# A gated conv-MLP's up-projection in a hybrid decoder layer: a seventh pair of weight tiles by half-size products, two granules of the down-projection's left operands parked in DRAM, and the last gate's loads and sums scheduled one by one

## The chip, the cores and the metric

The kernel runs on one core of a Trainium2 chip. The metric is device time in microseconds (us), the median of several runs. One execution was also recorded by the hardware profiler; all durations, idle times and clocks below come from that record. PE is TensorE, DVE is VectorE, ACT is ScalarE, POOL is GpSimd, SP is SyncE, which here only issues DMAs. A weight load of TensorE is listed as an engine of its own, PEld.

## The reference

One decoder layer in float32: 512 time steps, model width 1024, MLP width 2816. The change is in the second half:

```python
x = x + gate1 * mixer(adaln(x, c))           # HGRN2 and NSA heads, output projection
h = adaln(x, c)                              # rmsnorm, scale and shift from c @ w_ada + b_ada
u = causal_dwconv(h @ w_up, conv_w, conv_b)  # 1024 -> 2 x 2816, width-3 convolution in time
g = silu(u[..., :2816]) * u[..., 2816:]
x = x + gate2 * (g @ w_down)                 # 2816 -> 1024; gate2 is the sixth adaLN vector
```

`causal_dwconv` is `y[t] = b + u[t-2] w[0] + u[t-1] w[1] + u[t] w[2]` for each channel. The vector gate2 (1024 numbers) is one sixth of `c @ w_ada + b_ada`.

## The kernel before

**Products.** Each float32 product is made of three products of the short float type fp32r: an operand is split into `hi`, its rounded copy (ACT), and `lo`, the remainder (a subtraction, DVE), and `mm3` adds `hi*hi`, `hi*lo` and `lo*hi` (lines 155 to 157). Thus a float32 product is three matmuls.

**The up-projection.** `w_up` has 44 tiles of 128 output channels over K = 1024, which is 8 blocks of 128. Tiles are numbered so that 2f is a gate tile and 2f+1 the value tile with the same channels. A *plain* tile is 8 blocks x 3 = 24 matmuls with 512 columns (all time steps), into a PSUM bank `u`. A *pair* of tiles can also be made together by seven products of half size: K is cut into two halves, time into two halves of 256, the pair gives two tiles, and so the pair is a product of 2 x 2 blocks, for which seven block products do instead of eight. Each is 4 blocks x 3 = 12 matmuls with 256 columns, 84 for the pair, with sums and differences of the weights (tiles `wq`, `w3`) and of the activations (`hS`) as operands. DVE makes these differences; ACT and DVE split them; and between the products DVE adds what the banks share (tokens V, W, lines 1761 and 1763).

**Units.** `UNIT` is an order of tokens, written by hand, for four tiles: one pair by half products (P1 to P7) and two whole tiles (B0 B1 and C0 C1). The other tokens stand for one step each: `p` the post-processing of a finished tile (`up_post`: ACT scales and shifts at line 1623, two DVE additions of shifted copies at 1624 and 1625, ACT's silu at 1628 or DVE's multiplication at 1631); `n`, `f`, `s` the sums and splits of the next pair's weights; `m` the forms of whole tiles; `x` one step of a work list that prepares the left operands of the down-projection (`step(1)`); `g` one step of the generator `ada_last`, which computes gate2. A token with a prime is done for the next unit. `PRO` is the same kind of list for the first eight tiles. The loop runs `for j in range(NB, NU + 1)`, with `NB` = 2: units 2 to 7, tiles 8 to 31. In the last unit the primed tokens do nothing, but for two that prepare the first plain tiles. Tiles 32 to 43 are plain. `PLAIN` has a word for each of them: an A says that a tile prepared then is made with an accumulating transfer (below), and the last figure is how many steps of `ada_last` follow the tile.

**Loads.** `take` keeps three raw weight buffers filled (tag `raw`, 512 KB or 1 MB each); SP issues the next load when a buffer is freed, in program order, so loads wait behind each other. All SP loads go in one queue.

**The accumulating transfer.** Two of the whole tiles' `lo` parts per unit aren't made by DVE: ACT writes a negated copy (line 1684), POOL issues a DMA that adds the raw weights to it (line 1685), and PE uses the result as `wlo`.

**The last gate.** `ada_last` computes gate2 in two halves of 512. For each, it loads 8 blocks of `w_ada` of 128 x 512 (`ada2r`, 256 KB) with SP and adds each, weighted by a column of `cs`, to an accumulator (DVE, line 1407, the last of a half at 1410), then splits that and sums it over the 128 partitions with two small matmuls. Each `next(ada2)` runs up to the next `yield`: a sum of the previous block together with the load of the next.

**The down-projection** follows at about 565 us, also with products saved by sums of blocks. Its left operands come from `g`, in 11 granules j of two tiles. Each has parts `gP[j]` and `gQ[j]` (512 KB each, `hi` and `lo`), kept in SBUF, and `st34` and `st22`, which are written to DRAM (`pk34`, `pk22`) by ACT's DMA queue in `park` (lines 1835 and 1836) and read back by SP later (`load_s34`, line 1881). The first of its three phases calls `each_a(k)` behind every product k.

Of the kernel before, what the change touches and what calls it, by code (L numbers as in the profile page):

```python
# [10 lines left out]
F32 = mybir.dt.float32  # L11
F32R = mybir.dt.float32r
# [4 lines left out]
ALU = mybir.AluOpType  # L17
# [3 lines left out]
P = 128  # L21
# [3 lines left out]
KT = D // P  # L25
# [13 lines left out]
SCRATCH = 1024  # L39
LAG = 4  # L40
NB = 2
NU = 7
CUT = {"B": 6, "C": 7}
ADD = (1, 1)
PLAIN = "1 A3 A2 0 0 3 A2 2 A2 0 1 1"
PRO = ("t t g x M1 M2 t t t t F3 M3 F4 t A5 q0 M4 q1 q2 F6 q3 M5 M6 A7 x q4 g x q5 x t x n1' ns' f2' nc' n5' q6 na' g s4' m0' x x M7 m1' x f6' f7' x x x x f4'")
UNIT = ("P1 S P5 w n1' ns' x f3 B0 P6 P2 B1 x f2' V nc' n5' h1 x p-1 f4' P7 x m0' P3 h0' W p2 p0 na' C0 P4 x x x C1 s4' p1 x m1' x f6' x x x f7'")
PREP = ('sq2 sq3 rq2 rq3', '', 'nq0', 'fq0', 'nq1', '', 'lq0', 'fq1', 'nq2', '', 'lq1', 'fq2', 'nq3', 'lq2', 'fq3',
        'lq3', 'sk0 rk0 sk1 rk1', 'nk0 fk0 sk2 rk2', 'nk1 fk1 sk3 rk3', 'lk0 nk2 fk2', 'lk1 nk3 fk3 sa0 ra0',
        'sa1 ra1 lk2 na0 fa0', 'sa2 ra2 lk3 na1 fa1', 'sa3 ra3 la0 na2 fa2', '', 'la1 na3 fa3', '', 'la2', '', 'la3',  # L50
# [60 lines left out]
def hybrid_layer_kernel(ctx: ExitStack, tc: tile.TileContext, d: dict, out: bass.AP, dbg=None):  # L111
    nc = tc.nc
    ve, sc, gp, pe, sp = nc.vector, nc.scalar, nc.gpsimd, nc.tensor, nc.sync
# [7 lines left out]
    hbm = ctx.enter_context(tc.tile_pool(name="hbm", bufs=1, space=bass.MemoryType.DRAM))  # L121
# [4 lines left out]
    def nm(s):  # L126
        uid[0] += 1
        return f"{s}_{uid[0]}"

    def G(shape, dt=F32, s="g"):  # L130
        return gran.tile([P] + list(shape), dt, tag="g", name=nm(s))
# [4 lines left out]
    def TMP(shape, dt=F32, tag="tmp"):  # L136
        n = 1
        for a in shape[1:]:
            n *= a
        if n > 256:  # L140
            return tp.tile(shape, dt, tag="t2", name=nm(tag), bufs=9)
        return tp.tile(shape, dt, tag="t1", name=nm(tag), bufs=4)
# [4 lines left out]
    def f32(ap):  # L147
        return ap.bitcast(F32)
# [219 lines left out]
    cs = cst.tile([P, 8], F32, name="cs")  # L368
# [1026 lines left out]

    def ada_last(s, res):
        for q in range(2):
            acc = TMP([P, 512], tag="ada2")
            c0 = s * D + q * 512
            gp.memset(acc, 0.0)  # L1400
            sp.dma_start(acc[0:1], d["b_ada"][:, c0:c0 + 512])
            for k in range(KT):
                raw = TMP([P, 512], tag="ada2r")
                sp.dma_start(raw, ada_view[:, k, c0:c0 + 512])
                if k:
                    yield
                    ve.scalar_tensor_tensor(acc, last, cs[:, k - 1:k], acc, ALU.mult, ALU.add)
                last = raw
            yield
            ve.scalar_tensor_tensor(acc, last, cs[:, k:k + 1], acc, ALU.mult, ALU.add)  # L1410
            hi = TMP([P, 512], F32R, tag="rhi")
            lo = TMP([P, 512], F32R, tag="rlo")
            split(hi, lo, acc)
            yield
            ps = PS()
            pe.matmul(ps, onesr, hi, start=True, stop=False)
            pe.matmul(ps, onesr, lo, start=False, stop=True)
            sc.copy(res[:, q * 512:(q + 1) * 512], ps)
            yield


    x1 = []
# [183 lines left out]
    def up_mm(st, sl, ks=range(KT)):  # L1606
        if st not in us:
            us[st] = PS("u")
            if st not in wts:
                wts[st] = next_parts(st < nst - 2, added=st >= 4 * NU + 4 and PLAIN.split()[st - 4 * NU - 4][0] == "A")  # L1610
        hi, lo = wts[st]
# [4 lines left out]
    def up_post(st, silu=True):  # L1616
        f, s = divmod(st, 2)
        u = us.pop(st)
        if st >= 4 * NU + 3:
            step(3)  # L1620
# [94 lines left out]
    def banks(j):  # L1715
        us[4 * j + 1] = PS("u")
        us["x", j] = PS("ux")
        us[4 * j] = (held.pop if j == NU else held.get)(0)

# [5 lines left out]
    def do(j, tok):  # L1725
        last = j == NU
        if tok.endswith("'"):
# [66 lines left out]
    gQ = {}  # L1794
    evens = {}
    work = []
    h1, h2 = slice(0, 256), slice(256, 512)
    pk34 = hbm.tile([P, NJ, 2, 2, 256], F32, name="pk34")
    pk22 = hbm.tile([P, NJ, 2, 256], F32, name="pk22")

    def step(n):

        for _ in range(min(n, len(work))):
            fn, *a = work.pop(0)
            fn(*a)
# [26 lines left out]
                     (park, j, st22, st34)])  # L1832

    def park(j, st22, st34):
        sc.dma_start(pk22[:, j], f32(st22))
        sc.dma_start(pk34[:, j], f32(st34))

# [40 lines left out]
    def load_s34(j):  # L1878
        if j < NJ:
            S34[j] = G([2, 2, 256], F32R, s="S34")  # L1880
            sp.dma_start(f32(S34[j]), pk34[:, j])

    def load_a22(q):
        n = min(2, NJ - 2 * q)
# [42 lines left out]
    ada2 = ada_last(5, gt2)  # L1927
# [26 lines left out]
    made[0] = 1  # L1954
    for tok in PRO.split():
        if tok[0] == "M":
# [12 lines left out]
    made[0] = 1  # L1969
    for j in range(NB, NU + 1):  # L1970
        for tok in UNIT.split():
            do(j, tok)
    assert not tw
    first = 4 * NU + 4
    for st in range(first, nst):
# [5 lines left out]
        elif st > first + 1:  # L1981
            up_post(st - 2)
        for _ in range(int(PLAIN.split()[st - first][-1])):
            next(ada2, None)
# [29 lines left out]
    def each_a(k):  # L2014
        if k == 0:
            sc.activation(ys[nst - 2], ys[nst - 2], AF.Silu)
        elif k == 1:
            up_post(nst - 1)
        elif k % 2:
            step(3)  # L2020
        else:
            load_s34(k // 2 - 1)

# [27 lines left out]
    for q in range(NQ):  # L2051
        w = ready.pop(0)
# [7 lines left out]
    for a in range(2):  # L2060
        t = TMP([P, T])
        ve.tensor_tensor(t, bR[a], gt2[:, lead], ALU.mult)
        ve.tensor_tensor(rest[2 + a][:, lead], rest[2 + a][:, lead], t, ALU.add)
    for bank, a, cols in ((bS[0], 0, lead), (bS[1], 1, slice(0, 256)), (bV[0], 1, slice(256, 512))):
        for n, (hi, lo, j) in enumerate(ws):
            mm3(bank[:, cols], *stat(4, j, a), hi[:, cols], lo[:, cols], n == 0, n == len(ws) - 1)
        t = rest[2 + a][:, cols]
# [23 lines left out]
```

## Time and profile before

| | |
|---|---|
| median of 3 runs | 675.55 us (675.5 to 675.63) |
| the profiled execution, its own time | 675.78 us |
| its span, first to last instruction | 674.0 us |
| mean granted TensorE clock | 0.999 |
| up-projection's units, first to last matmul | 372.70 to 499.18 us |
| plain tiles | 499.18 to 565.38 us |
| HBM traffic | 103.96 MB read, 12.85 MB written |

A row of a timeline gives the start, the duration, the engine, the line of the code, the operation and its output and input; idle time of that engine just before it and what ended it stand in brackets. Matmuls overlap, so that a matmul's duration is longer than the distance to the next one. A row of windows gives, for each stretch, its length, then the busy time of each engine with the number of instructions, the granted clock, the DMA engines' busy share, and GB/s.

### The profile page before, as it was taken

What the parts mean: (1) busy time and instruction counts of PE and PEld (TensorE: products, weight loads), DVE (VectorE), ACT (ScalarE), POOL (GpSimd) and SP (SyncE); (2) the same over time, 40 slices, a digit from 0 to 9 for tenths busy, and PEclk for the clock granted to TensorE, in tenths of its full rate; (3) what the DMA queues carried; (4) which work ended last, traced back from release to release, by engine and by line L of the source; (5) the groups of instructions that cost most, each with busy time, mean ns of one, the idle gap of its engine ahead of it and who ended that gap; (6) DMA issues with size and microseconds to landing.
All of it is one profiled execution on the core that took longest, in us unless ns stands there. A gap on an engine that the chain in (4) does not pass through costs nothing.

```text
span 674.0 us, 10784 instructions
## 1 busy us (share of the span) xinstructions
PE 667.3 (99%) x3965; PEld 564.6 (84%) x3965; DVE 572.7 (85%) x1143; ACT 391.2 (58%) x751; POOL 60.0 (9%) x80
## 2 busy tenths in 40 slices
PE   8999999999999999999999999999999999999997
PEld 4668798788898889888998888989888888888886
DVE  5588988999998997687878988889888799988787
ACT  5564446666677688335665776667655555453431
POOL 1006144200000000200000011010101000000000
PEclk9999999999999999999999999999999999999999
DMA  9998444388042132435437567786689873959932
GB/s 284 284 323 266 143 157 136 104 287 256 10 148 95 33 107 103 167 103 154 156 94 188 150 172 178 205 231 168 160 222 224 247 248 135 377 205 399 382 111 93
DMA packets 109897, 126.43 MB, mean 188 GB/s; under 512 B 7003, under 2 KB 84627, under 8 KB 109845
## 3 DMA queue, kind: packets, MB, share of 16 engines
q1 hardware_dynamic: 103253, 105.84, 50.6%
q0 software_dynamic: 2448, 8.91, 7.0%
q10 hardware_dynamic: 4144, 10.99, 4.2%
q8 instruction: 31, 0.51, 0.3%
q14 instruction: 21, 0.17, 0.1%
HBM read 103.96 MB, written 12.85 MB: 173 GB/s over the span
## 4 chain that ended last, share of the span: by engine, by line
PE 89%; SPq 4%; DVE 3%; DMA 2%; issue 0%; ACT 0%; POOL 0%; DVEq 0%; POOLq 0%
PE u L156 11%; PE u L157 11%; PE u L155 11%; PE dn L156 5%; PE dn L157 5%; PE dn L155 5%; PE pT L155 3%; PE pT L157 3%; PE pT L156 3%; PE F L1056 3%; PE oT L1084 3%; SPq L316 2%; PE oh L157 2%; PE oh L155 2%; PE oh L156 2%; PE lev L1185 2%
## 5 line engine op out<-in xcount | busy, mean ns | idle before, releaser
L155 PE MATMUL u<-h2h,whi 128*128 128x512 f32 (+1 forms) x216 | 81.1, 375 | 0.0
L156 PE MATMUL u<-h2l,whi 128*128 128x512 f32 (+1 forms) x216 | 80.9, 375 | 0.0
L157 PE MATMUL u<-h2h,wlo 128*128 128x512 f32 (+1 forms) x216 | 80.7, 374 | 0.0
L152 DVE TENSOR_TENSOR wlo<-raw,whi 128x1024 fp32r<-128x1024 f32 (+1 forms) x37 | 43.3, 1170 | 6.9 <-ACT whi L151 6.7
L1624 DVE SCALAR_TENSOR_TENSOR y<-u,cv,y 128x511 f32<-128x511 f32 x44 | 32.8, 745 | 17.8 <-ACT y L1623 17.8
L157 PEld LDWEIGHTS u<-h2h,wlo 128*128 128x128 f32 x216 | 40.7, 188 | 7.7 <-DVE wlo L152 0.4
L155 PEld LDWEIGHTS u<-h2h,whi 128*128 128x128 f32 x216 | 40.8, 189 | 6.4
L156 PEld LDWEIGHTS u<-h2l,whi 128*128 128x128 f32 x216 | 40.8, 189 | 6.2
L151 ACT CAST whi<-raw 128x1024 fp32r<-128x1024 f32 (+1 forms) x37 | 37.2, 1005 | 14.9 <-PE kva L157 5.3
L1024 ACT ACTIVATE pt<-pt,mx 128x128 f32<-128x128 f32 (+3 forms) x64 | 35.9, 562 | 11.8 <-DVE mx L1008 10.8
L155 PE MATMUL pT<-hT,whi 128*128 128x512 f32 x96 | 39.2, 408 | 0.0
L157 PE MATMUL pT<-hT,wlo 128*128 128x512 f32 x96 | 37.7, 393 | 0.0
L156 PE MATMUL pT<-hT,whi 128*128 128x512 f32 x96 | 37.6, 391 | 0.0
L1628 ACT ACTIVATE y<-y 128x512 f32<-128x512 f32 x21 | 13.3, 632 | 39.8 <-DVE y L1625 39.8
L1008 DVE CUSTOM_DVE_ANT_0 pt<-S,cmask 128x128 f32<-128x128 f32 (+3 forms) x64 | 29.6, 484 | 6.4 <-PE S L1003 6.3
L1625 DVE SCALAR_TENSOR_TENSOR y<-u,cv,y 128x510 f32<-128x510 f32 x44 | 32.9, 748 | 1.6
L1063 ACT COPY pT<-F 128x512 f32<-128x512 f32 (+2 forms) x52 | 25.9, 502 | 14.4 <-PE F L1056 11.2
L1623 ACT ACTIVATE y<-u,cv 128x512 f32<-128x512 f32 x44 | 33.9, 772 | 0.2 <-PE u L157 0.2
L392 POOL TENSOR_TENSOR hrs<-hrs,mhalf 128x4 f32<-128x4 f32 (+2 forms) x16 | 20.0, 1258 | 136.4 <-DVE hrs L391 136.3
L156 PE MATMUL u<-h2l,w 128*128 128x512 f32 (+1 forms) x88 | 30.0, 341 | 0.0
L155 PE MATMUL u<-h2h,w 128*128 128x512 f32 (+1 forms) x88 | 30.0, 341 | 0.0
L157 PE MATMUL u<-h2h,w 128*128 128x512 f32 (+1 forms) x88 | 30.0, 341 | 0.0
(453 smaller groups left out, 2043.3 us busy)
## 6 DMA issues: line engine op xcount, KB each, us to landing
raw<-in_w_up SPq DMA_DIRECT2D x44, 512.0 KB, 5.1
aw<-in_w_ada SPq DMA_DIRECT2D x24, 512.0 KB, 3.6
raw<-in_w_down SPq DMA_DIRECT2D x10, 1024.0 KB, 5.5
ada<-in_w_ada SPq DMA_DIRECT2D x32, 256.0 KB, 6.1
wlo<-raw POOLq DMA_DIRECT2D x16, 512.0 KB, 5.1
raw<-in_w_in SPq DMA_DIRECT2D x7, 1024.0 KB, 6.3
rawd<-in_w_down SPq DMA_DIRECT2D x12, 512.0 KB, 10.2
pk<-st ACTq DMA_DIRECT2D x11, 512.0 KB, 3.1
```

Source lines behind the costliest of these rows:

```text
L151: sc.copy(hi, src)
L152: (eng or ve).tensor_tensor(lo, src, f32(hi), ALU.subtract)
L155: pe.matmul(o, ah, bh, start=start, stop=False, skip_group_check=True)
L156: pe.matmul(o, ah, bl, start=False, stop=False, skip_group_check=True)
L157: pe.matmul(o, al, bh, start=False, stop=stop, skip_group_check=True)
L1008: ve.tensor_tensor_reduce(pt[:, sl], ps[:, sl], cmask[:, 512 - W:512], -1.0, 1e30, ALU.add, ALU.min, mx[:, e:e + 1])
L1024: sc.activation(pt[:, sl], pt[:, sl], AF.Exp, bias=mx[:, e:e + 1], scale=-1.0, accum_out=su[:, h % 2, e:e + 1])
L1056: pe.transpose(ps[:, j * P:(j + 1) * P], src[:, j * P:(j + 1) * P], ident)
L1063: sc.copy(pT, ps[:, 0:n * P])
L1623: sc.activation(y, u, AF.Identity, bias=cv[:, 132 + c:133 + c], scale=cv[:, 88 + c:89 + c])
L1624: ve.scalar_tensor_tensor(y[:, 1:], u[:, :T - 1], cv[:, 44 + c:45 + c], y[:, 1:], ALU.mult, ALU.add)
L1625: ve.scalar_tensor_tensor(y[:, 2:], u[:, :T - 2], cv[:, c:c + 1], y[:, 2:], ALU.mult, ALU.add)
```

## The change

`NU` goes from 7 to 8: seven units, with tiles 8 to 35, and eight plain tiles, 36 to 43.

`AWAY = (0, 1)`: in `park`, the granules `gQ[0]` and `gQ[1]`, too, are written to DRAM (`pk26`) by ACT's queue and let go. They are read back by SP in the first phase of the down-projection, behind the products k = 3 and k = 5 (`load_away`).

`ada_last` adds directly into the result `gt2`, and a `g` is now either a load or a sum, not both. `PRO` has three more `g`, `UNIT` two (one that loads, behind P7, and one that sums, between p2 and p0), `PLAIN` four words less.

```diff
-NU = 7
+NU = 8
+AWAY = (0, 1)
...
-PLAIN = "1 A3 A2 0 0 3 A2 2 A2 0 1 1"
+PLAIN = "1 A2 A2 2 A2 2 1 1"
...
-UNIT = ("P1 S P5 w n1' ns' x f3 B0 P6 P2 B1 x f2' V nc' n5' h1 x p-1 f4' P7 x m0' P3 h0' W p2 p0 na' C0 P4 x x x C1 s4' p1 x m1' x f6' x x x f7'")
+UNIT = ("P1 S P5 w n1' ns' x f3 B0 P6 P2 B1 x f2' V nc' n5' h1 x p-1 f4' P7 x g m0' P3 h0' W p2 g p0 na' C0 P4 x x x C1 s4' p1 x m1' x f6' x x x f7'")
...
     def ada_last(s, res):
         for q in range(2):
-            acc = TMP([P, 512], tag="ada2")
+            acc = res[:, q * 512:(q + 1) * 512]
...
                 sp.dma_start(raw, ada_view[:, k, c0:c0 + 512])
-                if k:
+                yield
+                ve.scalar_tensor_tensor(acc, raw, cs[:, k:k + 1], acc, ALU.mult, ALU.add)
+                if k < KT - 1:
                     yield
-                    ve.scalar_tensor_tensor(acc, last, cs[:, k - 1:k], acc, ALU.mult, ALU.add)
-                last = raw
-            yield
-            ve.scalar_tensor_tensor(acc, last, cs[:, k:k + 1], acc, ALU.mult, ALU.add)
...
-            sc.copy(res[:, q * 512:(q + 1) * 512], ps)
-            yield
+            sc.copy(acc, ps)
...
     def park(j, st22, st34):
+        if j in AWAY:
+            sc.dma_start(pk26[:, AWAY.index(j)], f32(gQ.pop(j)))
         sc.dma_start(pk22[:, j], f32(st22))
...
+    def load_away(n):
+        if n < len(AWAY):
+            gQ[AWAY[n]] = G([2, 2, 256], F32R, s="gQ")
+            sp.dma_start(f32(gQ[AWAY[n]]), pk26[:, n])
...
         elif k % 2:
             step(3)
+            load_away(k // 2 - 1)
```

**Ahead of the first unit.** On DVE, the operands of the first unit's pair are split and summed: `wq` and `w` are weight forms, `e` is a sum of weights, `gP` a granule, `u` the bank sum of token V. Before:

```order
L152 TENSOR_TENSOR st_800_4165<-s_793_4146,st_800_4165 128x512
L152 TENSOR_TENSOR wq_4322<-raw_4094,wq_4322 128x512
L152 TENSOR_TENSOR w_831_4357<-raw_4245,w_831_4357 128x512
L1670 TENSOR_TENSOR e_4360<-raw_4245 128x512
L152 TENSOR_TENSOR wq_4364<-raw_4094,wq_4364 128x512
```

Now, on DVE at the same place (`gt` is the accumulator of gate2):

```order
L153 TENSOR_TENSOR st_798_4163<-s_791_4144,st_798_4163 128x512
L1407 SCALAR_TENSOR_TENSOR gt_3613<-ada2r_4264,cs,gt_3613 128x512
L153 TENSOR_TENSOR wq_4321<-raw_4092,wq_4321 128x512
L153 TENSOR_TENSOR w_829_4356<-raw_4243,w_829_4356 128x512
L1668 TENSOR_TENSOR e_4359<-raw_4243 128x512
L153 TENSOR_TENSOR wq_4364<-raw_4092,wq_4364 128x512
```

A sum of gate2 stands ahead of four operands that the first unit needs.

**In the units.** On DVE, the second unit, tokens W, p2 and p0 (`u` are banks, `y` the post-processed tiles). Before:

```order
L1763 TENSOR_TENSOR u_4550<-u_4550,w5u_4577 128x256
L1624 SCALAR_TENSOR_TENSOR y_4697<-u_4592,cv,y_4697 128x511
L1625 SCALAR_TENSOR_TENSOR y_4697<-u_4592,cv,y_4697 128x510
L1624 SCALAR_TENSOR_TENSOR y_4702<-u_3874,cv,y_4702 128x511
L1625 SCALAR_TENSOR_TENSOR y_4702<-u_3874,cv,y_4702 128x510
```

Now, on DVE:

```order
L1761 TENSOR_TENSOR u_4553<-u_4553,w5u_4580 128x256
L1622 SCALAR_TENSOR_TENSOR y_4703<-u_4596,cv,y_4703 128x511
L1623 SCALAR_TENSOR_TENSOR y_4703<-u_4596,cv,y_4703 128x510
L1407 SCALAR_TENSOR_TENSOR gt_3613<-ada2r_4680,cs,gt_3613 128x512
L1622 SCALAR_TENSOR_TENSOR y_4709<-u_3875,cv,y_4709 128x511
L1623 SCALAR_TENSOR_TENSOR y_4709<-u_3875,cv,y_4709 128x510
```

One sum stands between the two post-processings. SP's queue in the first units read `raw` loads alone before; now it is, on SP:

```order
L223 DMA raw_4267<-in_w_up 128x8x128 x2
L223 DMA raw_4353<-in_w_up 128x8x128 x2
L1405 DMA ada2r_4451<-in_w_ada 128x512
L223 DMA raw_4453<-in_w_up 128x8x128 x2
L223 DMA raw_4582<-in_w_up 128x8x128 x2
L1405 DMA ada2r_4680<-in_w_ada 128x512
L223 DMA raw_4682<-in_w_up 128x8x128 x2
```

One load of gate2's weights has come in for each unit, behind its two loads of 1 MB.

**In the down-projection's first phase.** On SP (`S` are the read-back sums `st34`, `rawd` and `raw` the weights). Before:

```order
L1881 DMA S_1089_6279<-pk_3610 128x1024
L222 DMA rawd_6293<-in_w_down 128x1024
L1881 DMA S_1095_6319<-pk_3610 128x1024
L222 DMA raw_6333<-in_w_down 128x2x1024
L222 DMA raw_6337<-in_w_down 128x2x1024
L1881 DMA S_1103_6366<-pk_3610 128x1024
```

Now, on SP:

```order
L1882 DMA S_1092_6340<-pk_3610 128x1024
L223 DMA rawd_6354<-in_w_down 128x1024
L1887 DMA gQ_6365<-pk_3612 128x1024
L1882 DMA S_1099_6382<-pk_3610 128x1024
L223 DMA raw_6396<-in_w_down 128x2x1024
L223 DMA raw_6400<-in_w_down 128x2x1024
L1887 DMA gQ_6414<-pk_3612 128x1024
L1882 DMA S_1109_6432<-pk_3610 128x1024
```

The first granule is read ahead of a read of sums, the second behind two weight loads.

More of the change, by code (lines that the diff above doesn't have):

```diff
@@ L41 @@
 NB = 2
-NU = 7
+NU = 8
+AWAY = (0, 1)
 CUT = {"B": 6, "C": 7}
 ADD = (1, 1)
-PLAIN = "1 A3 A2 0 0 3 A2 2 A2 0 1 1"
-PRO = ("t t g x M1 M2 t t t t F3 M3 F4 t A5 q0 M4 q1 q2 F6 q3 M5 M6 A7 x q4 g x q5 x t x n1' ns' f2' nc' n5' q6 na' g s4' m0' x x M7 m1' x f6' f7' x x x x f4'")
-UNIT = ("P1 S P5 w n1' ns' x f3 B0 P6 P2 B1 x f2' V nc' n5' h1 x p-1 f4' P7 x m0' P3 h0' W p2 p0 na' C0 P4 x x x C1 s4' p1 x m1' x f6' x x x f7'")
+PLAIN = "1 A2 A2 2 A2 2 1 1"
+PRO = ("t t g x M1 M2 t t t t F3 M3 F4 t A5 q0 M4 q1 q2 F6 q3 M5 M6 A7 x q4 g g x q5 x t x n1' ns' f2' nc' n5' q6 na' g g s4' m0' x x M7 m1' x f6' f7' x x x x g f4'")
+UNIT = ("P1 S P5 w n1' ns' x f3 B0 P6 P2 B1 x f2' V nc' n5' h1 x p-1 f4' P7 x g m0' P3 h0' W p2 g p0 na' C0 P4 x x x C1 s4' p1 x m1' x f6' x x x f7'")
 PREP = ('sq2 sq3 rq2 rq3', '', 'nq0', 'fq0', 'nq1', '', 'lq0', 'fq1', 'nq2', '', 'lq1', 'fq2', 'nq3', 'lq2', 'fq3',
@@ L1799, in hybrid_layer_kernel @@
     pk22 = hbm.tile([P, NJ, 2, 256], F32, name="pk22")
+    pk26 = hbm.tile([P, len(AWAY), 2, 2, 256], F32, name="pk26")
     def step(n):
```

## The prediction

> **What bounds the kernel now.** I read the head of the page first: who is busy, what the clock was, and which engine carries the chain that ended last.
>
> ```profile
> span 674.0 us, 10784 instructions
> PE 667.3 (99%) x3965; PEld 564.6 (84%) x3965; DVE 572.7 (85%) x1143; ACT 391.2 (58%) x751; POOL 60.0 (9%) x80
> PEclk9999999999999999999999999999999999999999
> PE 89%; SPq 4%; DVE 3%; DMA 2%; issue 0%; ACT 0%; POOL 0%; DVEq 0%; POOLq 0%
> ```
>
> PE is busy 667.3 of 674.0 us, at full clock in all slices, and the chain is PE for 89%. Since the change sits in the up-projection and in the start of the down-projection, I then asked for the windows of those stages. The cuts are starts of groups of matmuls: 372.70 to 499.18 holds the six units of four tiles (the first, fifth and sixth are shown), 499.18 to 520.95 the first four plain tiles, 543.20 to 565.38 the last four; the down-projection follows.
>
> ```profile
> core 0: us, PE busy (x) PEld busy (x) DVE busy (x) ACT busy (x) POOL busy (x), PEclk, DMA share, GB/s
> 372.70:394.05 21.35, 21.35 (x134) 19.00 (x133) 19.30 (x35) 15.51 (x27) 1.75 (x2) 1.00 0.73 185
> 457.13:478.15 21.02, 21.02 (x133) 19.07 (x132) 17.91 (x33) 13.80 (x25) 1.76 (x2) 1.00 0.74 188
> 478.15:499.18 21.03, 21.03 (x134) 19.07 (x132) 17.46 (x31) 12.98 (x24) 0.88 (x1) 1.00 0.80 211
> 499.18:520.95 21.77, 21.77 (x98) 18.02 (x96) 18.73 (x31) 12.20 (x20) 2.27 (x3) 1.00 0.79 191
> 543.20:565.38 22.18, 22.18 (x100) 18.36 (x99) 19.69 (x31) 11.56 (x18) 0.87 (x1) 1.00 0.60 193
> 570.00:592.00 22.00, 22.00 (x99) 18.22 (x98) 20.58 (x28) 11.98 (x19) 0.00 (x0) 1.00 0.97 364
> 592.00:604.00 12.00, 12.00 (x55) 9.93 (x54) 10.41 (x10) 6.37 (x8) 0.00 (x0) 1.00 0.45 161
> ```
>
> In each window PE's busy time equals the window's length. So the time here is the number of matmuls times their spacing, and everything else is only a condition: DVE, with 17 to 20 of 21 to 22 us busy, must keep handing over operands in time. The first unit takes 0.33 us more than the fifth (21.35 against 21.02), which is all the waiting that I can see in this stretch.
>
> **The change, part by part.** *The seventh pair.* Four plain tiles (4 tiles x 8 blocks x 3 products = 96 matmuls of 512 columns) become a unit: two plain tiles (48 of 512) and a pair by seven products (7 x 4 x 3 = 84 of 256). For the spacings, here are the first and the fourth of four matmuls that follow each other, of either size:
>
> ```profile
> 401.02 0.28 PE L155 MATMUL u<-hS,wq 128*128 128x256 f32 x1
> ...
> 401.38 0.28 PE L155 MATMUL u<-hS,wq 128*128 128x256 f32 x1
> ...
> 520.27 0.39 PE L155 MATMUL u<-h2h,w 128*128 128x512 f32 x1
> ...
> 520.95 0.39 PE L155 MATMUL u<-h2h,whi 128*128 128x512 f32 x1
> ```
>
> From start to start, three steps each, it is (401.38 - 401.02)/3 = 0.120 us with 256 columns and (520.95 - 520.27)/3 = 0.227 us with 512; the listed durations of 0.28 and 0.39 overlap. So 84 x 0.120 = 10.08 us stand against 48 x 0.227 = 10.90: 0.82 less. The windows, which hold the seams too, give 21.77 - 21.03 = 0.74 us. I take 0.74 and keep 0.82 as the other end.
>
> A rule of the Trainium skill speaks against this trade. "TensorE: Matmul & The Clock Gate", section "Back-to-back issue gap", says that in a sustained stream the weight load and the matmul set the spacing together, about 81 ns at 128 columns and 131 ns at 512; by an estimate between these (98 ns at 256) 84 matmuls would cost 8.2 us and 48 only 6.3, so the change would lose 1.9 us. Its formula for an isolated matmul gives 109 and 216 ns, and so a gain of 1.2 us; the rows above stand 11 ns over the formula at both sizes and contradict the sustained figures.
>
> *The adaLN sums between the units.* The vector is the same: 16 loads of 256 KB, 16 DVE sums, four small matmuls, the same copies. Only their places move. Before, the opening code had two sums and the units none; now the opening code has three, and each unit loads one block and sums one, between the two post-processings p2 and p0. What is there now:
>
> ```profile
> 452.24 0.75 DVE L1625 SCALAR_TENSOR_TENSOR y<-u,cv,y 128x510 f32<-128x510 f32 x1
> 454.42 0.75 DVE L1624 SCALAR_TENSOR_TENSOR y<-u,cv,y 128x511 f32<-128x511 f32 x1 [1.43 <-ACT y L1623]
> ...
> 453.08 0.63 ACT L1628 ACTIVATE y<-y 128x512 f32<-128x512 f32 x1 [2.09 <-DVE y L1625]
> 453.62 0.76 ACT L1623 ACTIVATE y<-u,cv 128x512 f32<-128x512 f32 x1
> ...
> L1407 DVE SCALAR_TENSOR_TENSOR ada<-ada2r,cs,ada 128x512 f32<-128x512 f32 x13 | 9.7, 748 | 0.2
> ```
>
> Ahead of p0, DVE stands idle for 1.43 us because ACT does the silu of p2 (453.08) and then p0's first step (453.62). A sum of 0.748 us fits into that hole with 0.68 to spare: cost nothing. If the hole were gone, it would be 0.75 us of DVE in a unit in which DVE has 3.1 to 3.6 us idle. In the last but one unit the end of the first half adds its split, in the last the two small matmuls, a copy and the start of the second half. These matmuls ran in the plain part before; moved, they cost the same. The plain tiles lose those sums and one accumulating transfer, so DVE reaches the down-projection no later than now.
>
> *The first unit* has the tightest place. The third sum comes ahead of its operand preparation (f4', n1', f3), where DVE has no idle time:
>
> ```profile
> 381.44 0.69 DVE L152 TENSOR_TENSOR wq<-raw,wq 128x512 fp32r<-128x512 f32 x1
> 383.07 0.43 DVE L1761 TENSOR_TENSOR u<-u,w5u 128x256 f32<-128x256 f32 x1
> 388.95 0.75 DVE L1624 SCALAR_TENSOR_TENSOR y<-u,cv,y 128x511 f32<-128x511 f32 x1 [0.47 <-ACT y L1623]
> 391.91 0.75 DVE L1624 SCALAR_TENSOR_TENSOR y<-u,cv,y 128x511 f32<-128x511 f32 x1 [1.43 <-ACT y L1623]
> ...
> 385.69 0.28 PE L155 MATMUL u<-h2h,wq 128*128 128x256 f32 x1
> ...
> 382.15 2.28 SPq L222 DMA_DIRECT2D raw<-in_w_up  x3
> ...
> 387.66 0.89 POOL L1685 DMA_DIRECT2D wlo<-raw  x1 [10.39 <-ACT wlo L1684]
> ...
> DMA to landing us min/median/max: 4.5/6.0/7.5
> ...
> 397.38 0.39 PE L157 MATMUL u<-h2h,wlo 128*128 128x512 f32 x1
> ...
> 382.60:390.70 8.10, 8.10 (x50) 7.23 (x49) 7.30 (x13) 4.51 (x7) 0.89 (x1) 1.00 1.02 263
> 390.70:395.20 4.50, 4.50 (x32) 4.14 (x31) 3.22 (x7) 2.84 (x6) 0.00 (x0) 1.00 0.56 113
> ```
>
> All of this moves 0.75 us back. The bank sum at 383.07 ends at 383.50, and the product that PE adds to what it has written starts at 385.69: 2.19 us of slack become 1.44. DVE gets the time back in the holes of 0.47 and 1.43. The second thing that moves is a load: the subtraction at 381.44 ends at 382.13 and frees a raw buffer, and SP issues the next weights at 382.15. Behind them, on the same DMA engines, POOL's accumulating transfer lands at 387.66 + 7.5 = 395.2 at the latest, and PE needs it at 397.38: 2.2 us of slack. Now it is 0.75 later and has one block of 256 KB more ahead of it, which at the 263 GB/s of that stretch takes 0.262/0.263 = 1.0 us: 395.2 + 1.75 = 396.95, or 0.43 before the need. I cost it at nothing; its bounds are a gain of 0 to 0.33 (the first unit loses its extra wait) and a loss that the second rival prices.
>
> *Two granules parked.* Of down's left operands, two of 512 KB each now leave through ACT's queue and come back through SP's during the first phase of the down-projection.
>
> ```profile
> 377.21 0.33 ACTq L1835 DMA_DIRECT2D pk<-st  x1
> ...
> S<-pk SPq DMA_DIRECT2D x11, 512.0 KB, 9.2
> ...
> 574.18 6.62 SPq L222 DMA_DIRECT2D raw<-in_w_down  x2
> 580.86 0.94 SPq L1881 DMA_DIRECT2D S<-pk  x2
> ...
> 595.30 0.39 PE L155 MATMUL dn<-w,gQ 128*128 128x512 f32 x1
> ```
>
> Two more issues on ACT cost 2 x 0.33 = 0.66 us of ACT in a stage where it has 6 us idle per unit. The reads add 1.05 MB; at the 364 GB/s of the window from 570 to 592, whose DMA share of 0.97 leaves no room, that is 2.9 us, and the next window has room (0.45). The later read stands behind the weights that SP issues from 574.18 and so is issued about 580.86; with the 9.2 us of the same kind of read and 2.9 us of crowding it lands at 593.0, before 595.30, where PE first uses a granule of its kind there (the parked ones are due about then or later). I cost it at nothing, by the window of 0.45, which shows room just ahead of the use. The other end is that all loads behind land 2.9 us later and none has slack: PE waits 2.9 us once, 677.7.
>
> *Sum:* 675.78 (the profiled execution; span 674.0 and 1.78 around it) - 0.74 = 675.04. That execution is 0.23 above the median of the runs, 675.55, so the median becomes 675.55 - 0.74 = **674.8 us**.
>
> **The rivals.**
> 1. *The saving is eaten by small waits (675.1 to 675.6).* Each unit's slack shrinks by some tenths; DVE is busy for 85%. With 0.3 to 0.8 us of such waits in all, two or three missed operands of the kind that costs the first unit 0.33 today, it is 675.1 to 675.6. Against it speaks that the later units show no wait at all, with a sum's room of 0.68 left beside the new sum.
> 2. *The accumulating transfer comes late (slower, 676.9).* If the extra block ahead of it costs its whole latency, the 3.0 us with which such a block lands here,
>
> ```profile
> ada2r<-in_w_ada SPq DMA_DIRECT2D x16, 256.0 KB, 3.0
> ```
>
> the first unit's transfer lands 3.75 us later against 2.2 us of slack: PE waits 3.75 - 2.2 = 1.6 us; the next unit has somewhat more slack and would wait some 0.5 more. 675.55 - 0.74 + 2.1 = 676.9. It decides from a delay of 2.2 us on; without 0.74 + 1.35 us of waits in all it isn't measurable as slower.
> 3. *The sums don't fit (slower, 680.0).* If the sum of each of the seven units stood in PE's way in full: 7 x 0.748 = 5.2 over 674.8. The idle 1.43 speaks against it.
> 4. *Half products spaced by their weight loads (slower, about 680).* A load of a 128x128 block is listed with 188 ns:
>
> ```profile
> L157 PEld LDWEIGHTS u<-h2h,wlo 128*128 128x128 f32 x216 | 40.7, 188 | 7.7 <-DVE wlo L152 0.4
> ```
>
> 84 x 0.188 = 15.8 against 10.9 would add 4.9 us, 680.4. The 0.120 between starts, in six units already, speaks against it. It is the kind of loss that the Trainium skill's sustained spacing would bring, with another size.
> 5. *More than 1.35 us faster.* That needs 0.6 us beside the saving, and the wait to be seen is 0.33.
>
> **How the numbers follow.** A measurement of this kernel can't tell 0.2%, 1.35 us, from no change. The forecast (674.4 to 675.1) has a chance of 0.69, rival 1 has 0.16: both are "the same". Rival 2 has 0.07, rivals 3 and 4 have 0.02 and 0.01; 0.01 stays for the parked granules' bound of 677.7, on the slow side. Rival 5 has 0.04. So faster 0.04, same 0.85, slower 0.11. The range goes from 675.55 - 0.82 - 0.33 = 674.4, rounded down to 674.3, up to rival 2, 676.9, which leaves out some 0.08 above (the upper half of rival 2, rivals 3 and 4, the bound of the granules) and 0.04 below.
>
> **What the profile after would show.** Seven units of 21.0 us from about 373, the last ending at about 520.2, and eight plain tiles to about 564.6; PE busy throughout all of these windows. Between p2 and p0 one DVE sum of 0.75 and an idle time of 0.7 behind it in the place of 1.43. The first whole tile of the second unit starting its third product without a wait for POOL's transfer. In the down-projection two more 512 KB reads on SP that land before PE's use, and the DMA share near 1.0 for 3 us longer. The prediction is wrong if PE has waits over 1 us in the units, most likely for the accumulated operand, or if the windows of the units come out longer than 21.1 us; and in the other direction if the plain tiles' spacing was held by something that I don't see.

## The result and the profile after

The changed kernel takes 684.96 us in the median (682.47 to 687.94), the kernel before, run beside it, 675.79: a ratio of 1.0133, 95% interval 1.0120 to 1.0145. It is 9.2 us slower, where 0.74 less was forecast. The profiled execution has 685.2 us and a span of 683.4.

The head of the page after:

```profile
span 683.4 us, 10876 instructions
PE 668.7 (98%) x4000; PEld 564.8 (83%) x4001; DVE 575.7 (84%) x1153; ACT 393.9 (58%) x759; POOL 61.2 (9%) x81
PE 66%; DVE 12%; DMA 8%; ACT 6%; SPq 5%; issue 2%; ACTq 0%; POOL 0%; DVEq 0%; POOLq 0%
```

PE is as busy as before (668.7 against 667.3 us). In the chain that ended last PE's share has fallen from 89% to 66%, and that of DVE, DMA and ACT together has risen from 5% to 26%. So there are new waits, and the windows by unit (cut at the start of each unit's P1; the first, second, fourth, sixth and seventh unit, the eight plain tiles, and the down-projection) say where:

```profile
373.88:395.18 21.30, 21.30 (x133) 18.99 (x132) 17.69 (x32) 15.00 (x26) 1.75 (x2) 1.00 0.81 215
395.18:420.56 25.38, 21.71 (x133) 18.96 (x132) 19.14 (x35) 14.19 (x25) 1.73 (x2) 1.00 0.71 188
442.92:464.74 21.82, 21.48 (x134) 18.98 (x133) 19.02 (x36) 14.28 (x25) 1.75 (x2) 1.00 0.76 194
486.42:510.06 23.64, 22.15 (x135) 19.33 (x134) 20.00 (x36) 16.25 (x28) 2.28 (x3) 1.00 0.72 181
510.06:531.09 21.03, 21.03 (x134) 19.07 (x132) 16.73 (x30) 12.12 (x21) 0.87 (x1) 1.00 0.75 200
531.09:575.07 43.98, 43.98 (x195) 36.41 (x194) 37.26 (x61) 24.37 (x39) 2.62 (x3) 1.00 0.70 217
575.07:680.22 105.15, 105.15 (x472) 87.05 (x470) 92.42 (x106) 45.98 (x56) 0.00 (x0) 1.00 0.72 269
```

The units and plain tiles together take 201.19 us, up to 575.07, where they took 192.64 before (372.74 to 565.38): 8.55 us more. Another 1.1 us of the difference between the two profiled executions lie ahead of the change: the up-projection's first matmul starts at 328.43 us against 327.29, and no edited line runs before it. In the profiles of the other kernels it starts anywhere from 326.57 to 328.06.

The first unit and the last take what they should, and so do the plain tiles and the down-projection. The second unit loses 4.35 us against 21.03, the fourth 0.8, the sixth 2.6 (of which 0.45 are the small matmuls moved there), and the two between them, from 420.56 to 442.92 and from 464.74 to 486.42, lose 1.3 and 0.65. The waits from 372 to 545 by engine and line name what DVE and PE waited for (in all, times, the longest):

```profile
DVE gt L1407 <- DMA ada2r<-in_w_ada: 17.7, 7, 5.0
PE u L156 <- ACT u L1755: 4.4, 3, 2.9
PE u L156 <- DVE u L1759: 2.1, 5, 0.7
```

Each unit's sum of gate2 stood waiting for its own block of weights. The timelines of DVE and SP (the two rows of DVE are those of the load of 388.22 and of the load of 436.07) and the landing time of the first such load:

```profile
397.61 0.75 DVE L1407 SCALAR_TENSOR_TENSOR gt<-ada2r,cs,gt 128x512 f32<-128x512 f32 x1 [5.05 <-DMA ada2r<-in_w_ada]
442.17 0.75 DVE L1407 SCALAR_TENSOR_TENSOR gt<-ada2r,cs,gt 128x512 f32<-128x512 f32 x1 [1.69 <-DMA ada2r<-in_w_ada]
...
388.22 2.85 SPq L1405 DMA_DIRECT2D ada2r<-in_w_ada  x1
...
431.72 4.31 SPq L223 DMA_DIRECT2D raw<-in_w_up  x4
436.07 1.73 SPq L1405 DMA_DIRECT2D ada2r<-in_w_ada  x1
...
DMA to landing us min/median/max: 9.4/9.4/9.4
```

In the third unit the token f3 frees a weight buffer, SP, which was blocked on it, issues four pieces of weights from 431.72 on, and comes to the block of gate2 at 436.07. DVE is at the sum at 442.17 - 1.69 = 440.48, only 4.4 us later. The block lands 6.1 us after its issue. In the first unit it is issued at 388.22 and lands after 9.4 us, and DVE, there since 392.56, waits for 5.05.

What stands behind the sum on DVE pays, and then ACT, and then PE. ACT and PE in the second unit:

```profile
399.90 0.63 ACT L1626 ACTIVATE y<-y 128x512 f32<-128x512 f32 x1 [5.95 <-DVE y L1623]
404.82 0.37 ACT L1755 COPY u<-u 128x256 f32<-128x256 f32 x1
...
405.25 0.39 PE L156 MATMUL u<-hS,wq 128*128 128x256 f32 x1 [2.93 <-ACT u L1755]
```

ACT's silu waits for p0 on DVE, the bank copy of token S comes ten instructions later, and PE's next product waits for that copy.

### The profile page after: what moved, and what is told of

Its sections match the earlier page's. It is cut to its first block, busy times and chain, and to the rows that moved or that the text cites. A ratio compares the mean times of both kernels' runs of the same rounds, so it can differ in the third digit from the quotient of the medians.

```text
span 683.4 us, 10876 instructions
## 1 busy us (share of the span) xinstructions
PE 668.7 (98%) x4000; PEld 564.8 (83%) x4001; DVE 575.7 (84%) x1153; ACT 393.9 (58%) x759; POOL 61.2 (9%) x81
## 4 chain that ended last, share of the span: by engine, by line
PE 66%; DVE 12%; DMA 8%; ACT 6%; SPq 5%; issue 2%; ACTq 0%; POOL 0%; DVEq 0%; POOLq 0%
PE dn L157 5%; PE dn L156 5%; PE dn L158 5%; DMA ada2r<-in_w_ada 5%; PE u L156 4%; PE u L158 4%; PE u L157 4%; PE pT L156 3%; PE pT L158 3%; PE pT L157 3%; PE F L1057 3%; PE oT L1085 3%; SPq L317 2%; PE oh L158 2%; PE oh L156 2%; PE oh L157 2%
## 5 line engine op out<-in xcount | busy, mean ns | idle before, releaser
L156 PE MATMUL u<-h2h,whi 128*128 128x512 f32 (+1 forms) x208 | 78.0, 375 | 0.0
L157 PE MATMUL u<-h2l,whi 128*128 128x512 f32 (+1 forms) x208 | 77.8, 374 | 0.0
L158 PE MATMUL u<-h2h,wlo 128*128 128x512 f32 (+1 forms) x208 | 77.6, 373 | 0.0
L158 PEld LDWEIGHTS u<-h2h,wlo 128*128 128x128 f32 x208 | 39.2, 188 | 7.5 <-DVE wlo L153 0.4
L156 PEld LDWEIGHTS u<-h2h,whi 128*128 128x128 f32 x208 | 39.3, 189 | 6.0
L157 PEld LDWEIGHTS u<-h2l,whi 128*128 128x128 f32 x208 | 39.3, 189 | 5.8
L156 PE MATMUL u<-hS,wq 128*128 128x256 f32 x84 | 24.5, 292 | 6.5 <-ACT u L1755 4.4
L157 PE MATMUL u<-h2l,w 128*128 128x256 f32 (+1 forms) x84 | 28.0, 333 | 0.0
L158 PE MATMUL u<-h2h,w 128*128 128x256 f32 (+1 forms) x84 | 28.0, 333 | 0.0
```

Of the source, the lines that this page charges most:

```text
L156: pe.matmul(o, ah, bh, start=start, stop=False, skip_group_check=True)
L157: pe.matmul(o, ah, bl, start=False, stop=False, skip_group_check=True)
L158: pe.matmul(o, al, bh, start=False, stop=stop, skip_group_check=True)
```

## The experiments

Three theories were set against each other: L (the loads come late, and that is all), D (the sums don't fit into DVE's time, whenever the data come), and O (units are a closed loop over DVE, SP, DMA and ACT, which has no slack). C (the loads' traffic) and P (the parking) are rivals for a part. The median of the kernel before beside these runs was 675.6 to 675.9 us.

**Sums without loads, loads without sums.** In `ada_last`, for the blocks of the units:

```diff
+                here = (q == 0 and k >= 3) or (q == 1 and k < 2)
+                if not here:
                     raw = TMP([P, 512], tag="ada2r")
                     sp.dma_start(raw, ada_view[:, k, c0:c0 + 512])
                 yield
-                ve.scalar_tensor_tensor(acc, raw, cs[:, k:k + 1], acc, ALU.mult, ALU.add)
+                ve.scalar_tensor_tensor(acc, acc if here else raw, cs[:, k:k + 1], acc, ALU.mult, ALU.add)
```

and for the second run

```diff
                 yield
+                if not here:
                     ve.scalar_tensor_tensor(acc, raw, cs[:, k:k + 1], acc, ALU.mult, ALU.add)
```

> The seven blocks of gate2's weights that the units load are not loaded; their seven sums stay where they are, and add the accumulator to itself (gate2 is another number by that). Theory L, the load comes late: DVE waits 17.7 us in all for these loads, and PE's 9.1 us of waits come behind it; without them the time is 674.8 to 675.6 us and PE's waits fall under 1 us. Rival D, the seven sums themselves don't fit into DVE's time: PE still waits about 0.5 us in each unit, 678 to 680. Rival P, the parked granules' writes crowd the first units: the 4.4 us of the second unit stay, about 679 to 680.

> The seven loads of the units stay, the seven sums that wait for them are left out (gate2 lacks these terms). Theory L: nobody waits for the loads, so 674.8 to 675.8 us. Rival C, the loads crowd the weights and the accumulating transfer: PE waits for weights or for the transfer, 677 or more, whatever DVE does. Rival D: as theory L.

Measured: 675.46 us without the loads (ratio 0.9995, 0.9986 to 1.0004) and 675.67 without the sums (0.9997, 0.9988 to 1.0006). PE's only waits from 372 to 545, of the first and of the second run:

```profile
PE u L156 <- DVE u L1761: 0.2, 1, 0.2
...
PE u L156 <- DVE u L1761: 0.3, 1, 0.3
```

Either half alone costs nothing that can be measured. That ends D and C as explanations of the 9 us, each by itself: seven sums fit, seven loads fit. It is the two together that cost, and the waits above show where: the sum waits for its load.

**The late loads without the seventh pair.** Twelve plain tiles again, with the changed kernel's `PRO`, `UNIT`, generator and parking.

```diff
-NU = 8
+NU = 7
-PLAIN = "1 A2 A2 2 A2 2 1 1"
+PLAIN = "1 A2 A2 0 2 2 A2 2 A2 0 1 1"
```

> The changed kernel's lists, generator and parking with the old number of units (NU 7, twelve plain tiles): the late loads without the seventh pair. Theory L: DVE waits for five or six late blocks, the units take as long as in the changed kernel, 25, 22.4, 21.8 and 21.7 us: 682 to 685 us. Rival: the seventh pair itself, with its 1 MB of weights forms, is what breaks the units: 675.5 to 677.

Measured: 686.0 us (1.0156, 1.0141 to 1.0172), 1.0 over the upper end of what was expected. DVE's waits from 372 to 545:

```profile
DVE gt L1407 <- DMA ada2r<-in_w_ada: 14.9, 6, 5.1
```

The loss comes with the lists, with six units as with seven; it doesn't need the seventh pair.

**The same load through another queue.** 

```diff
-                sp.dma_start(raw, ada_view[:, k, c0:c0 + 512])
+                gp.dma_start(raw, ada_view[:, k, c0:c0 + 512])
```

> Nothing is left out. The 256 KB loads of gate2's weights are issued by POOL's queue in place of SP's, at the same place of the program. POOL has nothing ahead of a unit's load but an accumulating transfer that was issued at 403.1 (second unit), so that the load goes out some 10 us earlier than the 414.2 at which SP gets to it behind four weight loads. Theory L: the loads land ahead of their sums, DVE waits under 1 us in all for them in the units, time 674.8 to 675.6. Rival D: DVE's waits go and PE's stay at about 0.5 us in each unit, 678 to 679. Rival C: 677 or more, with waits for POOL's accumulating transfers, which share that queue.

Measured: 681.23 us (1.0082, 1.0068 to 1.0096). DVE waits for no block any more, yet only 3.7 us of 9.2 came back. What is left is told by the rows of SP, ACT and DVE for the same unit (the third), first this kernel, then the kernel before, then the changed kernel:

```profile
427.89 5.71 SPq L223 DMA_DIRECT2D raw<-in_w_up  x4
433.94 1.06 ACT L1682 ACTIVATE wlo<-raw 128x1024 fp32r<-128x1024 f32 x1 [3.88 <-DMA raw<-in_w_up]
436.64 0.75 DVE L1622 SCALAR_TENSOR_TENSOR y<-u,cv,y 128x511 f32<-128x511 f32 x1 [2.52 <-ACT y L1621]
450.28 5.16 SPq L223 DMA_DIRECT2D raw<-in_w_up  x4
```

```profile
444.07 4.49 SPq L222 DMA_DIRECT2D raw<-in_w_up  x4
448.32 1.06 ACT L1684 ACTIVATE wlo<-raw 128x1024 fp32r<-128x1024 f32 x1 [2.08 <-DMA raw<-in_w_up]
446.15 0.43 DVE L1761 TENSOR_TENSOR u<-u,w5u 128x256 f32<-128x256 f32 x1 [1.16 <-PE u L157]
451.47 0.74 DVE L1624 SCALAR_TENSOR_TENSOR y<-u,cv,y 128x511 f32<-128x511 f32 x1
465.11 5.11 SPq L222 DMA_DIRECT2D raw<-in_w_up  x4
```

```profile
431.72 4.31 SPq L223 DMA_DIRECT2D raw<-in_w_up  x4
438.95 0.75 DVE L1622 SCALAR_TENSOR_TENSOR y<-u,cv,y 128x511 f32<-128x511 f32 x1 [1.00 <-ACT y L1621]
453.53 4.03 SPq L223 DMA_DIRECT2D raw<-in_w_up  x4
```

(The row of before is its fourth unit.) From one release of a buffer to the next there is a loop: f3 releases, the weights land, ACT makes its negated copy and then p2's first step, DVE does p2 and works from there to the next f3. In the kernel before it takes 7.40 us from the release to p2, and 13.64 from p2 to the next release: 21.04, PE's own time. This doesn't say that the loop has no slack, since PE sets the pace there: in the bank sum of token V, ahead of p2, DVE waits 1.16 us for PE (446.15), and at p2 it doesn't wait for ACT, whose first step for p2 ends at 450.99, 0.48 us earlier.

With POOL's loads p2 to release is again 13.64, so the sum does hide in its hole, but release to p2 is 8.75: 22.4 us, more than PE takes. The weights land later there: ACT's negated copy, which waits for them, starts 6.05 us after the release (433.94), where it was 4.25 before (448.32), and DVE waits 2.52 us for ACT. Why they land later isn't shown; the block is issued at 422.74, 5.15 us ahead of the release, and such a block lands after 5.6 us in the median. In the changed kernel release to p2 is 7.23, and p2 to release 14.58, longer by 0.94, which is about 1.69 + 0.75 - 1.43: 21.8 us.

The Trainium skill, "DMA: Bandwidth & Descriptors", section "Issuing engines are not separate DMA queues", says that transfers started by several engines run interleaved on the same 16 DMA engines, and that another issuer only saves issue time. The first half would fit the later weights, but no run here shows that the block is their cause. The second doesn't hold here: the issue on SP stood behind a blocked queue, and leaving that queue was worth 3.7 us.

**The sum elsewhere.** One run moves the sum from between p2 and p0 to behind p1, 8 us later. Another has POOL do it, with a multiplication and an addition (in the units; elsewhere DVE).

```diff
-... P7 x g m0' P3 h0' W p2 g p0 na' C0 P4 x x x C1 s4' p1 x ...
+... P7 x g m0' P3 h0' W p2 p0 na' C0 P4 x x x C1 s4' p1 g x ...
```

```diff
-                ve.scalar_tensor_tensor(acc, raw, cs[:, k:k + 1], acc, ALU.mult, ALU.add)
+                gp.tensor_scalar(raw, raw, cs[:, k:k + 1], None, ALU.mult)
+                gp.tensor_tensor(acc, acc, raw, ALU.add)
```

> Nothing is left out. The sum of each unit moves from between p2 and p0 to behind p1, some 8 us later; the load stays where it is and lands ahead of it (about 6 us after its issue at 414.2, against a sum at about 426). Theory L, only the late load costs: DVE's waits for it go and with them the loss, 674.8 to 675.8 us. Theory O, a loop binds: the release of a weight buffer (f3) sets the weight loads, these set ACT's negated copy and its next post-processing, and these set p2 on DVE, from which DVE works without a pause to the next f3; f3 to p2 takes 7.2 us, p2 to f3 13.64 without a sum on the way, 20.8 in all against PE's 21.03. A sum outside the hole adds 0.7, so 21.5 us a unit in spite of loads in time, 0.5 over PE's time in five or six units: 677 to 678.5 us.

> Nothing is left out. The sum of each unit is done by POOL (a multiplication and an addition) in place of DVE, so that POOL waits for the late load and DVE doesn't; loads as in the changed kernel. Theories L and O: p2 to f3 is 13.64 us again, the unit 21.0, the time 674.8 to 676. Rival D, the loads' traffic costs by itself: 677 or more. A rival of its own: POOL's work holds DVE up, DVE's operations get longer, 677 or more.

Measured: 680.78 us (1.0069, 1.0055 to 1.0083) and 686.06 us (1.0148, 1.0135 to 1.0161). Behind p1, DVE waits for no block, and from the third unit's V to the fifth's it takes 20.97 us a unit. Theory O had said 21.5 there, and missed: the sum outside the hole does lengthen p2 to release, to 14.30, but release to p2 is not fixed at 7.2 and was 6.66. Without a sum on the way the loop would take 6.66 + 13.64 = 20.3 us, by an estimate from these two, which is 0.7 less than PE's 21.03: so the loop is there, but it has slack. What is lost is lost elsewhere; the largest piece is a wait of PE of 2.3 us in the unit in which the first half of the vector ends, since ACT's rounded copy for the split stands in ACT's queue and waits for the late sum:

```profile
484.68 0.62 ACT L152 CAST rhi<-gt 128x512 fp32r<-128x512 f32 x1 [3.50 <-DVE gt L1407]
```

With the sums on POOL, ACT waits at that place for 4.1 us, and DVE loses time to POOL. POOL's rows, then DVE's, in the second unit:

```profile
417.47 1.56 POOL L1408 TENSOR_SCALAR ada2r<-ada2r,cs 128x512 f32<-128x512 f32 x1 [3.67 <-DMA ada2r<-in_w_ada]
419.12 1.35 POOL L1409 TENSOR_TENSOR gt<-gt,ada2r 128x512 f32<-128x512 f32 x1
...
419.24 1.52 DVE L1808 TENSOR_TENSOR s<-s,y 128x256 f32<-128x256 f32 x1
420.79 0.42 DVE L1808 TENSOR_TENSOR s<-y,s 128x256 f32<-128x256 f32 x1
```

DVE's subtraction at 419.24 takes 1.52 us beside POOL's addition, its twin right behind 0.42. The Trainium skill, "GPSIMD Engine Reference", section "1. Specifications", says that the two engines share their SBUF interface, with contention for DVE instructions with two SBUF inputs; this row agrees. The 686 us aren't accounted for in full.

**The load a unit ahead.** The block gets a buffer of its own (and the ring of temporaries one less), and is issued right behind the sum of the unit before. G stands for the small matmuls, and `PRO` has one more `g`, which loads the first unit's block. In the second run the own buffer serves the units alone, and the plain tiles' steps are set so that a load has a whole tile to land.

```diff
-... p-1 f4' P7 x g m0' P3 h0' W p2 g p0 ...
+... p-1 f4' P7 x G m0' P3 h0' W p2 g g p0 ...
...
-                raw = TMP([P, 512], tag="ada2r")
+                raw = tp.tile([P, 512], F32, tag="adr", name=nm("ada2r"), bufs=1)
...
-        return tp.tile(shape, dt, tag="t2", name=nm(tag), bufs=9)
+        return tp.tile(shape, dt, tag="t2", name=nm(tag), bufs=8)
```

> Nothing is left out. The blocks of gate2's weights have a buffer of their own (the ring of temporaries has eight in place of nine), and a unit's load is issued right behind the sum of the unit before, ahead of one of the two weight loads that SP is blocked on; the small matmuls of the first half stay at P7. SP issues it some 3.6 us earlier, and the sum comes as before between p2 and p0. Theory L: no waits for it, 674.8 to 675.8 us. Theory O: the sum hides in the hole, p2 to f3 is 13.64; f3 to p2 is 7.2 to 8.2 since the block now stands ahead of a weight load: 20.9 to 21.8 a unit, 675 to 678 us.

> Nothing is left out. As the run with the load a unit ahead, but the buffer of its own serves the loads of the units alone; in the plain tiles the blocks are temporaries as before, and each is loaded a whole tile ahead of its sum (steps 2 2 2 2 2 1 0 0). There the units took 21.1 us on average and the down-projection 110.1 us from its first product to its last matmul, where the kernel before takes 105.2, behind two waits of DVE for late blocks in the plain tiles. Theory L: with these gone as well, the down-projection is back at 105.2, and the time 675.0 to 675.7 us, 0.2 to 0.8 below the kernel before. Rival: the eight temporaries, or the parked granules' reads, hold the down-projection up: 678 or more.

Measured: 680.76 us (1.0077, 1.0064 to 1.0090), then, with the own buffer in the units only, 676.21 (1.0008, 0.9999 to 1.0017). The first run's units are mended already: PE has no listed wait from 372 to 565. Its loss is in the down-projection, behind DVE's waits for blocks in the plain tiles, where one buffer makes each load wait for the sum ahead. Of that run, DVE's waits from 525 to 600 and the window of the down-projection; then of the second run the third and the fourth unit and the down-projection:

```profile
DVE gt L1407 <- DMA ada2r<-in_w_ada: 12.3, 3, 5.4
...
565.69:675.75 110.06, 107.36 (x472) 87.88 (x470) 96.00 (x112) 49.11 (x62) 0.00 (x0) 0.98 0.70 264
```

```profile
415.85:437.20 21.35, 21.28 (x133) 18.99 (x132) 19.71 (x36) 14.29 (x25) 1.75 (x2) 1.00 0.79 203
437.20:458.22 21.02, 21.02 (x133) 19.07 (x132) 18.88 (x35) 14.29 (x25) 1.75 (x2) 1.00 0.76 199
565.82:671.24 105.42, 105.42 (x472) 86.99 (x470) 93.09 (x107) 45.96 (x56) 0.00 (x0) 1.00 0.71 269
```

With the blocks in time the whole change costs nothing that can be measured: the same sums and loads, with each load issued a unit ahead, take 676.21 in place of 684.96 us. With the two halves above, this run shows the cause. It doesn't gain either: 0.3 us stay in the third unit and 0.25 in the down-projection (105.42 against 105.17). From the up-projection's first matmul to the end this execution is 0.4 us shorter than the one before the change (346.36 against 346.72 us), but that matmul starts 0.8 us later (328.06 against 327.29). A saving of 0.74 us is smaller than the spread of that start.

**What the parking costs and what it is for.** The parking alone in the kernel before (its lines of the change, nothing else); the changed kernel without it; and, with the loads in time, granules 2 and 3 in place of 0 and 1.

```diff
-AWAY = (0, 1)
+AWAY = ()
```

```diff
-AWAY = (0, 1)
+AWAY = (2, 3)
```

> The kernel before with the parking alone: two granules written behind the first two units' products and read back in the first phase of the down-projection, NU 7 and the last gate as before. Theory L: no change, 675.3 to 676.1 us. Rival P: 1 to 4 us slower, with PE waits in the first two units; or a wait of up to 2.9 us in the down-projection, where the reads come late.

> The changed kernel without the parking: all granules stay in SBUF. Theories L and O: the waits of 1.7 us for the load in units three to six stay, 0.65 us a unit; the load of the first unit, whose landing took 9.4 us in the changed kernel while 512 KB more were written, lands sooner: 679 to 683 us. If parking has no part in it: 684 to 686. If parking is the main cause: 675 to 676.

> The same, but granules 2 and 3 are parked in place of 0 and 1, so that their 512 KB are written later, in the units three to five, and read back as the first of their phase. If the writes cost the 0.5 us that the third unit takes longer in the kernel with parking alone (21.63 against 21.03), wherever they fall: no difference, 675.0 to 675.7. If they cost since the first units are the tightest: 0.3 to 0.6 us less than the run before. If the granules' room is needed earlier: over 677.

Measured: 676.21 us (1.0003, 0.9994 to 1.0012), 691.21 (1.0227, 1.0214 to 1.0240) and 677.22 (1.0023, 1.0014 to 1.0033). By itself it can't be told from nothing; without it the changed kernel is slower still by 6 us, against every expectation, and later parking is worse by 1.0, just over the 677 that was expected if the room is needed earlier. There the third unit is back at 21.03, but the fourth and the fifth take 21.79 and 21.84; whether that is the room or the writes, this run doesn't tell. Left open by this was whether seven units need the room, and where the 0.74 had gone. So three runs have the kernel before with `NU = 8`, gate2's sums left in the plain tiles, and two, one or no granules parked:

```diff
-NU = 7
+NU = 8
+AWAY = (0, 1)
-PLAIN = "1 A3 A2 0 0 3 A2 2 A2 0 1 1"
+PLAIN = "2 A2 A3 2 A3 2 2 1"
```

> Nothing is left out. The kernel before with NU 8 and two granules parked; gate2's sums stay in the opening code and in the plain tiles, now 14 sums in eight tiles instead of twelve, and the units have none. If the units' loads and sums of gate2 ate the saving: 674.8 to 675.3 us. If the parking's writes ate it: the third unit takes 21.5 or more and the time is 675.3 to 676. Rival: eight tiles have no room on DVE for 14 sums (10.5 us, where DVE is idle for 3 us in four tiles), and DVE comes late into the down-projection: 677 to 680.

> The same with one granule parked. If the parking's writes cost, about half of their price comes back, and the third unit is at 21.0 to 21.3; if the second granule's room is needed, PE waits in the last units.

> The same with no granule parked. If the room isn't needed: the third unit takes 21.03 and the time is 674.6 to 675.2 us. If it is needed, as the run without parking seems to say, the last two units wait for buffers, some 2 to 6 us: 677 to 681.

Measured: 678.39 us (1.0041, 1.0027 to 1.0055), 680.80 (1.0074, 1.0061 to 1.0087) and 681.43 (1.0082, 1.0070 to 1.0095). The windows of the third and the last unit with two parked; of the third and the sixth with one; of the third, the sixth and the last with none:

```profile
415.04:436.61 21.57, 21.28 (x133) 18.98 (x132) 19.20 (x35) 14.29 (x25) 1.75 (x2) 1.00 0.74 186
499.69:520.72 21.03, 21.03 (x134) 19.07 (x132) 17.98 (x32) 13.50 (x24) 0.87 (x1) 1.00 0.83 211
```

```profile
414.60:435.63 21.03, 21.03 (x134) 19.08 (x133) 18.30 (x34) 14.28 (x25) 1.76 (x2) 1.00 0.74 188
477.68:500.91 23.23, 21.28 (x133) 18.99 (x132) 18.57 (x34) 14.61 (x26) 1.75 (x2) 1.00 0.66 170
```

```profile
414.44:435.47 21.03, 21.03 (x134) 19.08 (x132) 18.61 (x35) 14.61 (x27) 1.75 (x2) 1.00 0.73 188
477.52:499.56 22.04, 21.34 (x133) 18.92 (x132) 16.99 (x31) 13.74 (x24) 1.75 (x2) 1.00 0.72 179
499.56:522.39 22.83, 21.28 (x133) 18.99 (x132) 19.14 (x34) 13.48 (x24) 0.87 (x1) 1.00 0.71 185
```

Two parked granules cost 0.54 us in the third unit. One fewer brings that back and costs 2.2 in the sixth; none costs 1.0 and 1.8 in the last two. With one, ACT's split of weights waits in the sixth unit for a write of `st34` to DRAM, which holds a buffer that the split needs (ACT's waits from 480 to 530):

```profile
ACT wq L152 <- DMA pk<-st: 2.6, 1, 2.6
```

So the parking pays for the seventh unit's room, at a price of most of what the pair saves. That even the run with two granules is slower than before has the reason that the rival gave: DVE comes late. The down-projection takes 106.74 us there against 105.17, and the two longest of PE's waits from 372 to 676 are for the split of a half of gate2 behind its last sum, and for DVE's operands in the down-projection.

```profile
PE ps L1417 <- ACT rhi L152: 1.0, 1, 1.0
PE dn L157 <- DVE wlo L153: 0.9, 2, 0.5
```

So the sums do have to leave the plain tiles when these become eight.

**An eighth pair.** `NU = 9`, with the loads in time, a fourth sum ahead of the units, three granules parked.

```diff
-NU = 8
-AWAY = (0, 1)
-PLAIN = "2 A2 A2 2 A2 1 0 0"
+NU = 9
+AWAY = (0, 1, 2)
+PLAIN = "A2 2 A2 1"
-... A5 q0 M4 q1 q2 F6 ...
+... A5 q0 M4 q1 g g q2 F6 ...
```

> Nothing is left out. The same as the run ahead in units only, with an eighth pair (NU 9, four plain tiles), a fourth sum in the opening code and three granules parked. Theory: another 0.74 us less, 674.3 to 675.0, if the loads are all in time. Rival: four sums in the opening code and the loop of the units with no slack eat it, 675.5 to 678.

Measured: 683.04 us (1.0104, 1.0090 to 1.0118), above both expectations; PE waits for DVE's bank sum four times, 3.1 us in all, and 1.4 for the split ahead of the down-projection. No version that computes all of the layer beats the kernel before.

## Why the prediction was wrong

- **The step that failed is the price of the sums between the units:** "A sum of 0.748 us fits into that hole with 0.68 to spare: cost nothing." The hole is there, and a sum whose data are at hand does hide in it (675.46 us without the loads). But the sum's operand was taken as given. The load was costed for what stands behind it, the accumulating transfer, and never for its own arrival. Rows of the kernel before would have told: SP needs about 4.5 us for the four pieces of weights (444.07 + 4.49 = 448.56), and DVE is through with p2 at 452.24 + 0.75 = 452.99. The block had 4.4 us to land, where the page's median for the up-projection's weights is 5.1 us; the prediction's 3.0 for such a block is the median of 16 loads, of which none ran in the units. The block took 6.1 us, and DVE waited 1.7.
- **Every rival left it out.** Rival 3 came near in size (7 x 0.748), but argued from DVE's time. Rival 2 priced the same load's delay for the accumulating transfer, for which PE never waited in the changed kernel.
- **That "everything else is only a condition" was taken too lightly.** In the third and the fourth unit the wait of 1.7 us lengthens DVE's way from p2 to the next release by about 0.9 us, and PE loses 0.65 to 0.8 us in the fourth and the fifth: it keeps its 21.03 us only as long as the loop over f3, the weights, ACT and p2 takes no longer. That loop had some 0.5 to 0.7 us of slack (by the rows of the kernel before, and by the run behind p1). The prediction counted DVE's 3.1 to 3.6 us of idle time in a unit instead.
- **The first unit** was forecast as the tightest place, with up to 0.33 us to gain there. It takes 21.30 us, as before (21.31, counted from its first matmul at 372.74; the prediction's 21.35 counts from 372.70), and PE is busy throughout in both: this was no wait that the change could take away. The 5.05 us of DVE's wait at its end fall to the second unit.
- **The seventh pair's 0.74 us was right in kind:** units at 21.03 and plain tiles as before. The parking takes 0.54 of it back in the third unit, which was costed at nothing; its reads in the down-projection cost nothing, as forecast (105.15 against 105.17).
- **Not foreseen:** the sixth unit's loss, 2.2 us beside the moved matmuls. It follows ACT's split, which waits 1.77 us for the last sum of the first half (486.39). The split ends the fifth unit and its small matmuls stand in the sixth, each a unit earlier than the prediction has them.

## What to carry to other kernels

An instruction moved into a hole brings its operands along: for each load that moves, work out when its queue comes to it (behind which blocked issues), add a landing time from the same stretch, and hold that against the time at which the consumer's engine arrives. Where an engine at 99% shows no waits, look for loops of the other engines that take nearly as long as it does. The period alone doesn't tell, for while the busy engine sets the pace every loop shows its period (21.04 against 21.03 here); look for the rows in which the loop waits for it. The slack along such a loop, not an engine's idle share, says what a small delay costs. Where load and consumer may both be cheap alone, take either away, and then change their order alone.

## What was not expected of the hardware

A 256 KB load of 3.0 us to landing in the kernel before took 6.1 us behind four weight loads, and 9.4 in the first unit, with its issue alone 2.85 us on SP. A DVE subtraction of 0.42 us took 1.52 beside an addition on POOL. With the loads in POOL's queue no sum waited for a block, and yet ACT's negated copy began 6.05 us after a buffer's release, against 4.25 before; why is open.
